# RG-LRU gates with high and low parts stacked in rows, four PSUM buffers and tiles ten blocks apart

## The chip, the cores and the metric

The kernel runs on one core of a Trainium2 chip. The metric is the device time of one execution in microseconds (us), as the median over repeated runs. One core has several engines that work side by side, each through its own list of instructions in a fixed order: PE (matrix products, with weight loads shown as PEld), DVE (elementwise on vectors), ACT (activation functions, copies, casts), POOL (elementwise, slower) and SP, which here only issues DMA transfers. Engines wait for each other through semaphores. PE writes its results into PSUM, a small set of buffers that ACT or DVE must read before they are used again.

## The reference

One step of an encoder with two layers over 544 tokens (512 of a prompt, 32 of a second group), 1024 features. In each layer the input is projected, and three branches follow: softmax attention over chunks (A), retention (B) and a gated linear recurrence (C). Gated merges, a per-layer embedding and a layer norm close the layer. Branch C is what is changed:

```
def rg_lru(xr, s_conv, s_lru, conv_w, conv_b, w_gate_a, b_gate_a, w_gate_x, b_gate_x, lru_lambda):
    ...  # xc: causal convolution of width 4 over xr, plus conv_b; xb: xc in 8 blocks of 64 features
    r = jax.nn.sigmoid((jnp.einsum('btni,nij->btnj', xb, w_gate_a).reshape(b, t, w) + b_gate_a))
    ig = jax.nn.sigmoid((jnp.einsum('btni,nij->btnj', xb, w_gate_x).reshape(b, t, w) + b_gate_x))
    log_a = -LRU_C * r * jax.nn.softplus(-lru_lambda)
    ...  # a = exp(log_a); the input times ig times sqrt(1 - a^2); h = a * h_before + that, along time
```

The branch has 512 features, 8 blocks of 64, and each gate's weights are block-diagonal: a 64 x 64 matrix for each block.

## The kernel before

Activations lie with features in the 128 partitions (rows) and the 544 tokens along the columns. All weights are streamed from memory in blocks of 128 x 128, eight to a DMA (tile `raw`, 512 KB). Products keep nearly full fp32 precision by splitting both sides into a high part and the rest: ACT casts the high part (`wh` of weights, `xh` of activations, function `split` and `hilo`), DVE subtracts it (`wl`, `xl`), and PE adds three products, high x high, high x low, low x high, each in two pieces of 288 and 256 columns, so one block is six matmuls. `stream()` issues casts and subtractions of the blocks up to `LEAD` = 8 ahead of the one in use. SP issues the next `raw` when its buffer is free, which is when DVE's `wl` has read the old one.

The big projections run through a list of blocks in a fixed order. All other work is written as jobs (generators) which the block loop interleaves: each block is a tick, and a job that yields n goes on n ticks later. The table `PACE` holds these distances. So the numbers in `PACE` set the place of each job's instructions between the blocks, the same on each engine, and every engine then runs its list in that order.

Jobs that matter here, in one layer:

- `lru_tile(t)`, t = 0 to 3 (128 features each): convolution (`xc`), its high and low part (`xch`, `xcl`, 128 x 547), then for each of the two gates six matmuls of 274 columns into two PSUM buffers (`sc` and `pv`), and on ACT three sigmoids out of them (`lru_r` for gate a, `lru_i` for gate x). The weights' tile of a gate has two 64 x 64 blocks on the diagonal and zeros elsewhere. POOL multiplies `lru_i` by `xc`.
- `lru_job`, started when tile 3 is done: for four tiles `lru_a` and `lru_r` on ACT (exp, tanh), then three operations on DVE ("trio"), a square root on ACT, a product on POOL, and two scans on DVE (prompt and second group).
- `va_job`/`tok_steps`: the values `VA` are transposed on PE in five "flips" of four transposes each into the PSUM buffer `tp`, and ACT copies each to `vatok`, one flip every three blocks.
- `attn_job`: SP loads two bias tiles (`bias`), POOL masks a corner of each (memset), PE multiplies `KT` and `QT` into `sc`, DVE adds the bias and takes a minimum (`exps`, shown as ISA or CUSTOM_DVE_ANT_0), ACT takes the exponential (`sx`), DVE divides (`norm`), PE transposes into `tp` again. It starts when the gates, `vatok` and the first keys are there.

PSUM has two buffers `mm` for the block products, two `sc`, one `tp` and one `pv`. Before the first block, `busy(WARM)` runs matmuls on zeros, and `ple_split` casts the per-layer embedding (`phl`), whose products come first.

Of the kernel before, what the change touches and what calls it, by code (L numbers as in the profile page):

```python
# [17 lines left out]
NP, NS = 512, 32  # L18
# [37 lines left out]
def blocks_of(kind):  # L56
# [8 lines left out]
LEAD = 8  # L65

HELD = (6, 2)
WARM = 16

PACE = {  # L70
# [5 lines left out]

# [10 lines left out]

P_CW, P_CB, P_BA, P_BX, P_LAM, P_GN, P_LG, P_LB = 0, 16, 20, 24, 28, 32, 36, 44
P_SC, P_SL = 52, 64
P_S0 = 68  # L90
NPAR = P_S0 + 256


# [30 lines left out]
def encoder(ctx: ExitStack, tc, xT, pT, W, RB, KC, VC, PAR, CST, LGB, o_y, o_k, o_v, o_rp, o_rs, o_cv, o_lr):  # L124
# [47 lines left out]

    def tick():
        clock[0] += 1
        stream()
        for j in list(jobs):
            while j[1] <= clock[0]:
                d = next(j[0], None)
                if d is None:
                    jobs.remove(j)  # L180
                    break
                j[1] = clock[0] + d
# [98 lines left out]

    def ple_split(l):
        pr, p2 = ple_in[l]
        for k in range(2):
            hilo(p2[:, k], p2[:, 2 + k], pr[:, k])

    V.memset(zero.bitcast(F32), 0.0)
    busy(WARM)
# [32 lines left out]
    def layer(l, env, nxt):  # L321
        pa = par[l]

        def pcol(c, t):
            return pa[:, c + t:c + t + 1]
# [171 lines left out]

        def lru_tile(t):
            if t == 0:
                env["lru"] = [sl("lru_r"), sl("lru_i"), sl("lru_a")]  # L500
            R, I, _ = env["lru"]
            xrp = env["xrp"]
            xc = tmp("xc", (128, W547))
            S.activation(xc, xrp[:, t, 0:W547], AF.Identity, scale=pcol(P_CW, t), bias=pcol(P_CB, t))
            for j in range(1, 4):
                V.scalar_tensor_tensor(xc, xrp[:, t, j:j + W547], pcol(P_CW + 4 * j, t), xc, MUL, ADD)
            yield PACE["lt1"]
            xch, xcl = (tp_.tile([128, W547], F32R, tag="tmp", name="xch") for _ in range(2))
            hilo(xch, xcl, xc)
            yield PACE["lt2"]  # L510
            for g in range(2):
                w, lo = ([parts[(l * NB + AT["wg"] + g * 4 + t) // 4][i][:, t] for i in range(2)])
                ps = psum("sc"), psum("pv")
                for i, (wg, x) in enumerate(((w, xch), (w, xcl), (lo, xch))):
                    for p_, c0 in ((ps[0], 0), (ps[1], W547 - 274)):
                        T.matmul(p_[:, :274], lhsT=wg, rhs=x[:, c0:c0 + 274], start=i == 0, stop=i == 2)  # L516
                d = (I if g else R)[:, t]
                b_ = pcol(P_BX if g else P_BA, t)
                S.activation(d[:, :274], ps[0][:, :274], AF.Sigmoid, bias=b_)
                S.activation(d[:, 274:NP], ps[1][:, 1:NP - 273], AF.Sigmoid, bias=b_)  # L520
                S.activation(d[:, NP:], ps[1][:, 274 - NS:274], AF.Sigmoid, bias=b_)
                yield PACE["lt3"]
            G.tensor_tensor(I[:, t, :NP], I[:, t, :NP], xc[:, :NP], MUL)
            G.tensor_tensor(I[:, t, NP:], I[:, t, NP:], xc[:, NP + 3:], MUL)
            if t == 3:
                env["gates"] = True
                add(lru_job())

        def lru_job():
            R, I, A = env["lru"]  # L530

            for t in range(4):
                S.activation(A[:, t], R[:, t], AF.Exp, scale=sp[:, 1, l, t:t + 1])
                S.activation(R[:, t], R[:, t], AF.Tanh, scale=sp[:, 0, l, t:t + 1])
                yield PACE["lru0"]
            y = I
            for t in range(4):
                r, a = R[:, t], A[:, t]
                V.scalar_tensor_tensor(r, a, 1.0, r, ADD, MUL)
                V.tensor_scalar(a, r, -1.0, 1.0, MUL, ADD)  # L540
                V.scalar_tensor_tensor(r, a, 1.0, r, ADD, MUL)
                yield PACE["lru1"]
            for t in range(4):
                S.activation(R[:, t], R[:, t], AF.Sqrt)
                yield PACE["lru2"]
            for t in range(4):
                G.tensor_tensor(R[:, t], R[:, t], I[:, t], MUL)
                yield PACE["lru3"]
                V.tensor_tensor_scan(y[:, t, :NP], A[:, t, :NP], R[:, t, :NP], 0.0, MUL, ADD)
                V.tensor_tensor_scan(y[:, t, NP:], A[:, t, NP:], R[:, t, NP:], pcol(P_SL, t), MUL, ADD)  # L550
            yield 2
            env["yc"] = y
            Q.dma_start(out=o_lr[l, :, :, 0:1], in_=y[:, :, NP - 1:NP])
            Q.dma_start(out=o_lr[l, :, :, 1:2], in_=y[:, :, N - 1:N])
# [290 lines left out]
        def evac(kind, t, ps, hf=None):  # L845
# [36 lines left out]
            elif kind == "xr":  # L882
                if t == 0:
                    env["xrp"] = xrp = sl("xrp", shape=(128, 4, N + 6))
                    V.memset(xrp[:, :, 0:3], 0.0)
                    V.tensor_copy(xrp[:, :, NP + 3:NP + 6], pa[:, P_SC:P_SC + 12].rearrange("p (a b) -> p a b", a=4))
                xrp = env["xrp"]
                S.copy(xrp[:, t, 3:3 + NP], pv[:, :NP])
                S.copy(xrp[:, t, NP + 6:], pv[:, NP:])  # L889
                if t == 3:  # L890
                    Q.dma_start(out=o_cv[l, :, :, 0:3], in_=xrp[:, :, NP:NP + 3])
                    Q.dma_start(out=o_cv[l, :, :, 3:6], in_=xrp[:, :, NP + NS + 3:NP + NS + 6])
                add(lru_tile(t), PACE["lt00"] if t == 1 else PACE["lt0"])
            elif kind in ("za", "zb", "zc"):
                for f in {"za": ("ya1", "ya2"), "zb": ("yb",), "zc": ("yc",)}[kind]:
                    need(env, f)
                y = env["y" + kind[1]]
                if t == 0:
                    env[kind] = (sl(kind + "h", F32R), sl(kind + "l", F32R))
                h, lo = env[kind]  # L900
                z = tmp("z")
                S.activation(z, pv, AF.Sigmoid)  # L902
                if kind == "zb":
                    V.scalar_tensor_tensor(z, pv, pcol(P_GN, t), z, MUL, MUL)
                else:
                    V.tensor_tensor(z, pv, z, MUL)
                V.tensor_tensor(z, z, y[:, t], MUL)
                hilo(h[:, t], lo[:, t], z)
            elif kind[0] == "g":
                sg = tmp("sg")  # L910
                S.activation(sg, pv, AF.Sigmoid)  # L911
                env["sg", t] = sg
            elif kind[0] == "b":
                sg = env.pop(("sg", t))
                a, b = t // 4, t % 4
                if kind == "bC":
                    if b == 0:
                        env["m", a] = sl("m")
                    V.tensor_tensor(env["m", a][:, b], pv, sg, MUL)
                else:  # L920
                    V.tensor_tensor(sg, pv, sg, MUL)  # L921
                    m = env["m", a][:, b]
                    (V if kind == "bB" and t == 7 else G).tensor_tensor(m, m, sg, ADD)  # L923
                    if kind == "bB":
                        if b == 0:
                            env["mh", a], env["ml", a] = sl("mh", F32R), sl("ml", F32R)
                        hilo(env["mh", a][:, b], env["ml", a][:, b], m)
            elif kind == "pl":
                if t % 4 == 0:
                    env["ple", t // 4] = sl("ple")  # L930
                S.copy(env["ple", t // 4][:, t % 4], pv)  # L931
            elif kind == "wo":
                a, b = t // 4, t % 4
                if b == 0:
                    env["r", a] = sl("r")
                r, xh_, xl_ = env["r", a][:, b], st["xh"][a][:, b], st["xl"][a][:, b]
                V.scalar_tensor_tensor(r, xh_.bitcast(F32), ALPHA, pv, MUL, ADD)
                V.scalar_tensor_tensor(r, xl_.bitcast(F32), ALPHA, r, MUL, ADD)  # L938
                hilo(xh_, xl_, r)
            elif kind == "pg":  # L940
                if t == 7 and hf and l == L - 1:
                    for _ in gate(t, ps, hf):
                        pass
                else:
                    add(gate(t, ps, hf), 0)
# [92 lines left out]

    with tc.manual_schedule():
        envs = [{} for _ in range(L + 1)]  # L1040
        stream(2)
        ple_split(0)
        add(x_job(envs[0]), PACE["x"])
        for l in range(L):
# [84 lines left out]
```

## Time and profile before

| | |
|---|---|
| median of 3 runs | 1309.9 us (1309.42 to 1310.03) |
| profiled execution | 1309.81 us, span 1308.0 |
| PE busy | 1291.7 us, 10744 matmuls |
| DVE busy | 717.3 us |
| ACT busy | 546.1 us |
| POOL busy | 177.0 us |
| matmuls of the gates (line 516) | 96, in both layers |
| HBM read | 112.57 MB |

The span is the time from the first to the last instruction of the profiled execution. A row of the timeline gives start, duration, engine, line, operation, output <- inputs with the tile's shape, and in brackets the idle time before it with what ended it. Rows of equal kind that follow each other are drawn together (x2, x3).

### The profile page before, as it was taken

The numbers are of one execution on the slowest core, as the hardware profiler recorded it, in microseconds if no ns is written. First come the engines' busy times: TensorE is split into PE (matmuls) and PEld (weight loads), VectorE is DVE, ScalarE is ACT, GpSimd is POOL, SyncE is SP. The second block draws the span as 40 slices with busy tenths as digits, with TensorE's granted clock in tenths as the row PEclk, the third lists the DMA queues.
The fourth block names the chain that finished last, engine by engine and source line by source line (L and its number), as shares of the span: only waits on it lengthen the run. The fifth ranks groups of instructions, "written<-read, shape, count | busy, mean of one in ns | idle before, by whom it ended". The sixth has DMA issues, their size and how long they took to land.

```text
span 1308.0 us, 25456 instructions
## 1 busy us (share of the span) xinstructions
PE 1291.7 (99%) x10744; PEld 1263.5 (97%) x10744; DVE 717.3 (55%) x1271; ACT 546.1 (42%) x1065; POOL 177.0 (14%) x158
## 2 busy tenths in 40 slices
PE   9999999999999999999999999999999999999996
PEld 9999999999999999999989998999999999999996
DVE  5666662573753453465584756626637444434567
ACT  6665544323632232333277655443235322332231
POOL 0210120410101201000032201224001011010000
PEclk9999999999999999999999999999999999999998
DMA  7233522231222222224112335222222222222231
GB/s 282 66 131 98 171 69 80 85 105 50 85 93 82 97 68 94 97 97 146 65 49 66 131 99 166 74 83 82 89 66 81 95 83 86 92 81 97 81 113 69
DMA packets 43457, 125.90 MB, mean 96 GB/s; under 512 B 9360, under 2 KB 11664, under 8 KB 42576
## 3 DMA queue, kind: packets, MB, share of 16 engines
q1 hardware_dynamic: 43344, 124.29, 28.8%
q8 instruction: 84, 1.38, 0.4%
q14 instruction: 29, 0.24, 0.1%
HBM read 112.57 MB, written 7.24 MB: 92 GB/s over the span
## 4 chain that ended last, share of the span: by engine, by line
PE 95%; DVE 3%; DMA 1%; ACT 1%; issue 0%; SPq 0%; POOL 0%; DVEq 0%
PE mm L254 84%; PE pv L432 2%; PE sc L402 2%; PE tp L418 1%; PE tp L330 1%; DMA raw<-in_W 1%; PE sc L661 1%; PE pv L684 1%; PE pv L516 0%; DVE r L813 0%; PE sc L516 0%; DVE xl L263 0%; PE sc L744 0%; PE sc L597 0%; PE pv L679 0%
## 5 line engine op out<-in xcount | busy, mean ns | idle before, releaser
L254 PE MATMUL mm<-xh,wh 128*128 128x288 f32 x2144 | 455.5, 294 | 0.4 <-ACT xrp L889 0.4
L254 PE MATMUL mm<-xh,wl 128*128 128x288 f32 x2144 | 444.1, 288 | 0.0
L254 PE MATMUL mm<-xl,wh 128*128 128x288 f32 x2144 | 442.7, 288 | 0.0
L210 DVE TENSOR_TENSOR wl<-raw,wh 128x512 fp32r<-128x512 f32 (+1 forms) x354 | 261.4, 756 | 283.8 <-ACT wh L209 279.9
L254 PEld LDWEIGHTS mm<-xh,wh 128*128 128x128 f32 x2144 | 328.3, 189 | 10.7 <-issue 7.4
L254 PEld LDWEIGHTS mm<-xl,wh 128*128 128x128 f32 x2144 | 328.8, 188 | 0.0
L254 PEld LDWEIGHTS mm<-xh,wl 128*128 128x128 f32 x2144 | 328.5, 188 | 0.2 <-DVE wl L210 0.2
L209 ACT CAST wh<-raw 128x512 fp32r<-128x512 f32 (+1 forms) x354 | 208.3, 614 | 36.9 <-PE mm L254 30.8
L911 ACT ACTIVATE sg<-mm 128x544 f32<-128x544 f32 x48 | 30.1, 626 | 154.1 <-PE mm L254 154.1
L923 POOL TENSOR_TENSOR m<-m,sg 128x544 f32<-128x544 f32 x30 | 46.8, 1560 | 316.6 <-DVE sg L921 316.6
L355 ACT ACTIVATE sx<-sx,sst 128x128 f32<-128x128 f32 (+4 forms) x68 | 38.0, 559 | 70.1 <-DVE sst L353 66.0
L254 PE MATMUL mm<-xh,held 128*128 128x288 f32 (+1 forms) x320 | 64.0, 291 | 0.3 <-ACT ple L931 0.3
L254 PE MATMUL mm<-ml,wh 128*128 128x288 f32 (+1 forms) x256 | 52.9, 288 | 0.0
L254 PE MATMUL mm<-mh,wl 128*128 128x288 f32 (+1 forms) x256 | 52.6, 286 | 0.0
L254 PE MATMUL mm<-mh,wh 128*128 128x288 f32 (+1 forms) x256 | 52.5, 286 | 0.0
L254 PEld LDWEIGHTS mm<-xh,held 128*128 128x128 f32 x320 | 51.3, 188 | 0.6 <-ACT ple L931 0.5
L254 PE MATMUL mm<-xl,held 128*128 128x288 f32 (+1 forms) x160 | 46.4, 290 | 0.5 <-DVE xl L263 0.5
L262 ACT CAST xh<-r 128x544 fp32r<-128x544 f32 (+2 forms) x32 | 17.0, 532 | 67.8 <-DVE r L938 63.6
L921 DVE TENSOR_TENSOR sg<-mm,sg 128x544 f32<-128x544 f32 x32 | 23.2, 725 | 36.7 <-PE mm L254 36.7
L565 POOL TENSOR_TENSOR swap<-swap,cst 128x544 f32<-128x544 f32 x16 | 25.3, 1580 | 109.8 <-DMA swap<-QB 68.1
L902 ACT ACTIVATE z<-mm 128x544 f32<-128x544 f32 x24 | 15.0, 626 | 59.2 <-PE mm L254 59.1
L254 PEld LDWEIGHTS mm<-mh,wl 128*128 128x128 f32 x256 | 39.3, 188 | 0.0
(251 smaller groups left out, 1791.9 us busy)
## 6 DMA issues: line engine op xcount, KB each, us to landing
raw<-in_W SPq DMA_DIRECT2D x189, 512.0 KB, 3.3
bias<-in_RB SPq DMA_DIRECT2D x16, 256.0 KB, 4.1
x<-in_xT SPq DMA_DIRECT2D x4, 544.0 KB, 9.2
o_v<-VA SPq DMA_DIRECT2D x2, 1088.0 KB, 5.1
o_k<-KT SPq DMA_DIRECT2D x2, 1088.0 KB, 5.1
swap<-KB SPq DMA_DIRECT2D x32, 68.0 KB, 2.0
swap<-QB SPq DMA_DIRECT2D x32, 68.0 KB, 2.0
o_y<-tk SPq DMA_DIRECT2D x6, 256.0 KB, 2.1
```

What stands on the lines that cost most here:

```text
L209: S.copy(h[:, k:k + step], t)
L210: V.tensor_tensor(lo[:, k:k + step], t, h[:, k:k + step].bitcast(F32), SUB)
L254: T.matmul(ps[:, MM0 + a:MM0 + b], lhsT=w[:, n % 4, :], rhs=x[:, a:b], start=first and i == 0, stop=last and i == 2)
L262: S.copy(h, src)
L355: S.activation(x, x, AF.Exp, bias=s[:, 0:1], scale=-1.0, accum_out=s[:, 1:2])
L402: T.matmul(scs[j][:, o:o + n], lhsT=q_[r, p, i * 128:i * 128 + 128], rhs=k_[r, p, :n], start=k == 0, stop=k == 2)
L432: T.matmul(pv[64 * j:64 * j + 64, i * 128:i * 128 + 128], lhsT=env["vatok"][:, kt, h * 64:h * 64 + 64], rhs=xs[j][:, o:o + 128], start=kt ...
L565: G.tensor_tensor(sw, sw, cst[:, C_SIN:C_SIN + N], MUL)
L902: S.activation(z, pv, AF.Sigmoid)
L911: S.activation(sg, pv, AF.Sigmoid)
L921: V.tensor_tensor(sg, pv, sg, MUL)
L923: (V if kind == "bB" and t == 7 else G).tensor_tensor(m, m, sg, ADD)
```

## The change

The gates' weights are laid out densely: for each block of 64 features one tile holds [gate a | gate x] side by side (64 x 128), twice below each other in the rows. On the other side the rows are the high part of one half of a tile's features and the low part of the same half. One matmul then adds high x high and low x high in one pass, and with the weights' low part it adds the rest. A tile needs, for each half, two matmuls in two pieces: 8 instead of 12. Half 0 goes to the two `sc` buffers, half 1 to `pv` and `tp`. Each PSUM buffer now holds gate a in 64 rows and gate x in the other 64, so ACT reads it in pieces of 64 rows, 8 for a tile instead of 6; the cast and the subtraction of `xc` also go in two halves of 64 rows. All tiles of the recurrence are 547 columns wide (the three between the two groups are carried along), and POOL's product is one instead of two.

`PACE` puts the tiles about ten blocks apart and has `lru_job` go on every 2 ticks, not 3. At the start, weights are cast at most two blocks ahead for the first eight blocks, `WARM` is 14, and the first embedding half is cast in two pieces.

```
-WARM = 16
+WARM = 14
...
-    "sa3": 3, "lt0": 2, "lt00": 8, "lt1": 8, "lt2": 5, "lt3": 3, "lru0": 3, "lru1": 3, "lru2": 1, "lru3": 3,
+    "sa3": 3, "lt0": (2, 13, 15, 17), "lt1": 8, "lt2": 5, "lt3": 3, "lru0": 2, "lru1": 2, "lru2": 1, "lru3": 3,
...
-        stream()
+        stream(LEAD if clock[0] > 8 else 2)
...
         for k in range(2):
-            hilo(p2[:, k], p2[:, 2 + k], pr[:, k])
+            for a, b in SPANS if l == 0 and k == 0 else ((0, N),):
+                hilo(p2[:, k, a:b], p2[:, 2 + k, a:b], pr[:, k, a:b])
...
-            xch, xcl = (tp_.tile([128, W547], F32R, tag="tmp", name="xch") for _ in range(2))
-            hilo(xch, xcl, xc)
+            xs = [tp_.tile([128, W547], F32R, tag="tmp", name="xhl") for _ in range(2)]
+            rows = slice(0, 64), slice(64, 128)
+            for b in range(2):
+                S.copy(xs[b][rows[b]], xc[rows[b]])
+            for b in range(2):
+                V.tensor_tensor(xs[b][rows[1 - b]], xc[rows[b]], xs[b][rows[b]].bitcast(F32), SUB)
             yield PACE["lt2"]
-            for g in range(2):
-                w, lo = ([parts[(l * NB + AT["wg"] + g * 4 + t) // 4][i][:, t] for i in range(2)])
-                ps = psum("sc"), psum("pv")
-                for i, (wg, x) in enumerate(((w, xch), (w, xcl), (lo, xch))):
+            for b in range(2):
+                n = l * NB + AT["wg"] + 2 * t + b
+                ps = [psum(k) for k in (("pv", "tp") if b else ("sc", "sc"))]
+                for i in range(2):
                     for p_, c0 in ((ps[0], 0), (ps[1], W547 - 274)):
-                        T.matmul(p_[:, :274], lhsT=wg, rhs=x[:, c0:c0 + 274], start=i == 0, stop=i == 2)
-                d = (I if g else R)[:, t]
-                b_ = pcol(P_BX if g else P_BA, t)
-                S.activation(d[:, :274], ps[0][:, :274], AF.Sigmoid, bias=b_)
-                S.activation(d[:, 274:NP], ps[1][:, 1:NP - 273], AF.Sigmoid, bias=b_)
-                S.activation(d[:, NP:], ps[1][:, 274 - NS:274], AF.Sigmoid, bias=b_)
+                        T.matmul(p_[:, :274], lhsT=parts[n // 4][i][:, n % 4], rhs=xs[b][:, c0:c0 + 274],
+                                 start=i == 0, stop=i == 1)
+                for d, r, b_ in ((R, rows[b], P_BA), (I, rows[1 - b], P_BXS)):
+                    b_ = pcol(b_, t)[r]
+                    S.activation(d[rows[b], t, :274], ps[0][r, :274], AF.Sigmoid, bias=b_)
+                    S.activation(d[rows[b], t, 274:], ps[1][r, 1:274], AF.Sigmoid, bias=b_)
                 yield PACE["lt3"]
-            G.tensor_tensor(I[:, t, :NP], I[:, t, :NP], xc[:, :NP], MUL)
-            G.tensor_tensor(I[:, t, NP:], I[:, t, NP:], xc[:, NP + 3:], MUL)
+            G.tensor_tensor(I[:, t], I[:, t], xc, MUL)
...
-                add(lru_tile(t), PACE["lt00"] if t == 1 else PACE["lt0"])
+                add(lru_tile(t), PACE["lt0"][t])
...
-        stream(2)
+        stream(1)
         ple_split(0)
```

How the instructions move, counted in blocks from a layer's first: the gate products stood in groups of six at blocks 46, 49, 52, 54, 55, 57, 62 and 65; they stand in groups of four at 46, 49, 57, 60, 67, 70, 77 and 80. The flips stay at 84, 87, 90, 93 and 96, the first attention products at 105, the transposes of softmax weights at 113, 116 and 121.

On ACT, at the first flips, before (`vatok<-tp` is the copy of a flip; the numbers tell buffers apart):

```order
L533 ACTIVATE lru_a_474<-lru_r_472,sp_92 128x544
L534 ACTIVATE lru_r_472<-lru_r_472,sp_92 128x544
L855 COPY VA_746<-mm_913 128x544
L209 CAST wh_981<-raw_798 128x512
L209 CAST wh_1012<-raw_798 128x512
L331 COPY vatok_1021<-tp_1023 128x512
L331 COPY vatok_1021<-tp_1050 128x512
L879 ACTIVATE QTh_1062<-mm_980 128x544
```

And in the changed order, from the copy of flip 0 on, behind the second pair of `lru_a` and `lru_r`:

```order
L335 COPY vatok_1003<-tp_1005 128x512
L542 ACT_TABLE_LOAD
L542 ACTIVATE lru_a_474<-lru_r_472,sp_92 128x547
L543 ACTIVATE lru_r_472<-lru_r_472,sp_92 128x547
...
L335 COPY vatok_1003<-tp_1033 128x512
L888 ACTIVATE QTh_1045<-mm_957 128x544
L890 ACTIVATE qs_1047<-mm_957 128x32
L211 CAST wh_1053<-raw_842 128x512
```

The table load and the pairs of all four tiles stood ahead of the flips' copies; now they stand between them: tiles 0 and 1 between copies 0 and 1, tile 2 between copies 1 and 2, tile 3 between copies 2 and 3.

On DVE, from the keys' low part (`KTl`) to the first softmax (ISA), before:

```order
L263 TENSOR_TENSOR KTl_1149<-KT_1146,KTh_1148 128x544
L860 COPY kn_1065<-mm_1069 128x32
L210 TENSOR_TENSOR wl_1155<-raw_950,wh_1154 128x512
L210 TENSOR_TENSOR wl_1191<-raw_950,wh_1190 128x512
L549 SCALAR_TENSOR_TENSOR lru_i_473<-lru_a_474,lru_r_472 128x512
...
L880 SCALAR_TENSOR_TENSOR QTl_1063<-mm_1153,QTh_1062 128x544
L210 TENSOR_TENSOR wl_1236<-raw_1016,wh_1235 128x512
L353 ISA sx_1249,sst_1263<-sc_1247,bias_1200 128x128
```

And in the changed order (`raw_919` there is what `raw_950` was):

```order
L265 TENSOR_TENSOR KTl_1136<-KT_1133,KTh_1135 128x544
L869 COPY kn_1048<-mm_1052 128x32
L212 TENSOR_TENSOR wl_1142<-raw_919,wh_1141 128x512
L548 SCALAR_TENSOR_TENSOR lru_r_472<-lru_a_474,lru_r_472 128x547
L549 TENSOR_SCALAR lru_a_474<-lru_r_472 128x547
L550 SCALAR_TENSOR_TENSOR lru_r_472<-lru_a_474,lru_r_472 128x547
...
L212 TENSOR_TENSOR wl_1182<-raw_919,wh_1181 128x512
L889 SCALAR_TENSOR_TENSOR QTl_1046<-mm_1140,QTh_1045 128x544
L212 TENSOR_TENSOR wl_1225<-raw_1001,wh_1224 128x512
L357 ISA sx_1239,sst_1253<-sc_1237,bias_1189 128x128
```

All four trios stood ahead of `KTl`; now those of tiles 0 and 1 stand just ahead of it and those of tiles 2 and 3 ahead of the second `wl`. The scans of tiles 0 and 1, which stood ahead of the softmax, now come in the places of tiles 2 and 3, and the scans of tiles 2 and 3 ahead of the next pair's weights.

SP's list at the bias tables, in the changed order:

```order
L203 DMA raw_1001<-in_W 128x1024
L203 DMA raw_1095<-in_W 128x1024
L203 DMA raw_1185<-in_W 128x1024
L347 DMA bias_1189<-in_RB 128x512
L347 DMA bias_1191<-in_RB 128x512
L203 DMA raw_1284<-in_W 128x1024
```

It reads as before, and nothing moved here: the bias tables stand behind the `raw` that takes the buffer of `raw_919` (of `raw_950` before), and so behind DVE's last `wl` from it.

More of the change, by code (lines that the diff above doesn't have):

```diff
@@ L89 @@
 P_SC, P_SL = 52, 64
-P_S0 = 68
+P_BXS = 68
+P_S0 = 72
 NPAR = P_S0 + 256
@@ L499, in lru_tile @@
             if t == 0:
-                env["lru"] = [sl("lru_r"), sl("lru_i"), sl("lru_a")]
+                env["lru"] = [sl(k, shape=(128, 4, W547)) for k in ("lru_r", "lru_i", "lru_a")]
             R, I, _ = env["lru"]
@@ L535, in lru_job @@
                 yield PACE["lru0"]
-            y = I
+            y = I[:, :, :N]
             for t in range(4):
@@ L549, in lru_job @@
                 V.tensor_tensor_scan(y[:, t, :NP], A[:, t, :NP], R[:, t, :NP], 0.0, MUL, ADD)
-                V.tensor_tensor_scan(y[:, t, NP:], A[:, t, NP:], R[:, t, NP:], pcol(P_SL, t), MUL, ADD)
+                V.tensor_tensor_scan(y[:, t, NP:], A[:, t, NP + 3:], R[:, t, NP + 3:], pcol(P_SL, t), MUL, ADD)
             yield 2
@@ L1068 @@
             if kind == "wg":
-                W[l, n // 8, :, n % 8] = 0
-                for b in range(2):
-                    r = slice(64 * b, 64 * b + 64)
-                    W[l, n // 8, r, n % 8, r] = g["w_gate_x" if k // 4 else "w_gate_a"][l, 2 * (k % 4) + b]
+                ax = [g[a][l, k] for a in ("w_gate_a", "w_gate_x")]
+                W[l, n // 8, :, n % 8] = np.tile(np.concatenate(ax[::-1] if k % 2 else ax, 1), (2, 1))
                 continue
@@ L1094 @@
             put(c, feat(g[k][l], t))
+        put(P_BXS, np.roll(feat(g["b_gate_x"][l], 4), 64, 0))
         put(P_SC, feat(g["state_conv"][l, 0], 4))
```

## The prediction

> **What bounds the kernel now.** I read the page's head, clock row and chain first, then the timelines of the three places that the change touches.
>
> ```profile
> span 1308.0 us, 25456 instructions
> PE 1291.7 (99%) x10744; PEld 1263.5 (97%) x10744; DVE 717.3 (55%) x1271; ACT 546.1 (42%) x1065; POOL 177.0 (14%) x158
> PEclk9999999999999999999999999999999999999998
> PE 95%; DVE 3%; DMA 1%; ACT 1%; issue 0%; SPq 0%; POOL 0%; DVEq 0%
> ```
>
> PE is busy for 99% of the span and carries 95% of the chain. Two things follow: a matmul that is taken away is worth its own time, and a new wait of PE is paid in full, since there is no slack left to swallow it. The profiled execution took 1309.81 us, 0.1 below the median of 1309.9, with 1.8 outside the span; I sum against 1309.8.
>
> **The start.** Timeline from the beginning (start, duration, engine, line, what; in brackets the idle time before and its releaser):
>
> ```profile
> 1.20 4.00 PE L269 MATMUL mm<-zero 128*128 128x272 f32 x16 [1.20 <-DVE eps L289]
> 4.59 1.30 ACT L262 CAST phl<-pr 128x544 fp32r<-128x544 f32 x2
> 5.29 1.52 PE L254 MATMUL mm<-phl,wh 128*128 128x288 f32 x4
> 7.62 0.71 ACT L209 CAST wh<-raw 128x256 fp32r<-128x256 f32 x2 [1.74 <-DMA raw<-in_W]
> 8.87 0.62 ACT L209 CAST wh<-raw 128x512 fp32r<-128x512 f32 x1 [0.53 <-DMA raw<-in_W]
> 9.40 1.12 ACT L931 COPY ple<-mm 128x544 f32<-128x544 f32 x2
> 10.05 0.77 PE L254 MATMUL mm<-phl,wh 128*128 128x288 f32 x4 [0.71 <-ACT ple L931]
> 11.68 0.72 DVE L263 TENSOR_TENSOR xl<-x,xh 128x544 fp32r<-128x544 f32 x1
> ```
>
> The first product at 5.29 waits for a cast of 544 columns (half of the 1.30 at 4.59); with the cast cut in two it needs the first piece, about 0.3 sooner, and two warm-up matmuls fewer (4.00 / 16 = 0.25 each) are out of the way by then. At 10.05 PE waits for ple, whose copy stood on ACT behind a weight cast that waited for its DMA. With weights two blocks ahead that cast comes behind the copy, which can start when the pair at 7.62 is done (8.33); this takes away the 0.71, up to 0.9 with the weight load's part. Later weights, cast nearer to their use, can cost small waits where a DMA lands late: I put 0.2 against it. Gain 1.0; bounds 0.3 (the first cast alone) and 1.2.
>
> **The gate products.** PE in the middle of a tile's second gate, and the wait that the answer for line 516 lists (total, times):
>
> ```profile
> 52.76 0.29 PE L516 MATMUL sc<-xch,held 128*128 128x274 f32 x1
> ...
> 53.27 0.42 PE L254 MATMUL mm<-xh,wh 128*128 128x288 f32 x2
> ```
>
> ```profile
>   ACT lru_r L521: 0.6, 2
> ```
>
> From 52.76 to 53.27 four matmuls pass, 0.128 each. 32 of the 96 go: 4.1. Twice a gate waited for ACT to read the other gate's buffer; with four buffers and tiles ten blocks apart (7.5 us at six matmuls of 0.126) these 0.6 go too. Gain 4.7, bounds 4.1 and 4.7. Against this a tile costs ACT one more cast and eight sigmoid pieces for six, DVE one subtraction more. The table by stretch (PE, PEld, DVE, ACT, POOL busy) around the gates:
>
> ```profile
> 34.00:64.00 30.00, 29.90 (x238) 29.69 (x236) 18.97 (x33) 19.93 (x47) 5.96 (x6) 1.00 0.24 71
> ```
>
> No row shows 547 columns on 64 partitions; the bounds are half and all of the 128-partition prices, 0.65 and 0.72, and I take all. With some 1.3 for the sigmoids that is 2 us of ACT and 0.7 of DVE a tile, once in 7.5 us, where ACT idles 10 of 30 us and DVE 11. I cost it at nothing; without that cover it would be 2 us a tile at most. Sum so far -5.7, or 1304.1, if nothing new waits.
>
> **What moves.** Tile 3 of the recurrence now finishes at block 80 instead of 65. The work behind it (lru_a and lru_r on ACT, three DVE operations a tile, then root, product, scan) starts where PE transposes VA, one flip every three blocks from 84 to 96. PE's own places of flips and attention stay. F is flip 0's start on PE, 77.46.
>
> ```profile
> 69.64 0.75 ACT L533 ACTIVATE lru_a<-lru_r,sp 128x544 f32<-128x544 f32 x1
> 72.50 0.60 ACT L209 CAST wh<-raw 128x512 fp32r<-128x512 f32 x1
> 77.46 0.60 PE L330 MATMUL tp<-cst,VA 128*128 128x128 f32 x4
> 78.09 0.59 ACT L331 COPY vatok<-tp 128x512 f32<-128x512 f32 x1 [1.79 <-PE tp L330]
> 81.55 0.63 ACT L879 ACTIVATE QTh<-mm 128x544 fp32r<-128x544 f32 x1 [0.16 <-PE mm L254]
> 82.85 0.60 PE L330 MATMUL tp<-cst,VA 128*128 128x128 f32 x4
> 85.12 1.28 ACT L544 ACT_TABLE_LOAD   x1
> ```
>
> *Step 1, the flips.* tp has one buffer, so flip n+1 waits for ACT's copy of flip n. On ACT there now stand between copy 0 and copy 1 a table load (1.28) and the lru pairs of two tiles (72.50 - 69.64 = 2.86). Copy 0 ends at F+1.2, the load F+2.5, the pairs F+5.4, copy 1 F+6.0. Flip 2 stands at 82.85 - 77.46 = 5.4 and waits 0.65. Then QTh, QTl on DVE, qs and a cast (to F+8.0), tile 2's pair (F+9.4), copy 2 (F+10.0). Flip 3 stands at 8.1 + 0.65 and waits 1.3. Copy 3 ends at F+12.4, flip 4 is due at F+12.7. A layer 1.9, bounds 1.3 (the detour over DVE hidden) and 2.5 (as much more).
>
> *Step 2, the first softmax.* DVE, POOL, SP and PE behind it, and the stretch's busy times:
>
> ```profile
> 76.42 0.72 DVE L539 SCALAR_TENSOR_TENSOR lru_r<-lru_a,lru_r 128x544 f32<-128x544 f32 x1
> 78.29 0.68 DVE L210 TENSOR_TENSOR wl<-raw,wh 128x512 fp32r<-128x512 f32 x1
> 87.22 4.00 POOL L547 TENSOR_TENSOR lru_r<-lru_r,lru_i 128x544 f32<-128x544 f32 x3 [21.16 <-ACT lru_r L544]
> 89.87 1.93 DVE L263 TENSOR_TENSOR KTl<-KT,KTh 128x544 fp32r<-128x544 f32 x1 [2.57 <-ACT KTh L262]
> 91.82 1.28 DVE L210 TENSOR_TENSOR wl<-raw,wh 128x512 fp32r<-128x512 f32 x2
> 93.02 1.21 DVE L549 TENSOR_TENSOR_SCAN lru_i<-lru_a,lru_r 128x512 f32<-128x512 f32 x1
> 93.12 0.33 SPq L201 DMA_DIRECT2D raw<-in_W  x1
> 93.50 0.91 SPq L343 DMA_DIRECT2D bias<-in_RB  x2
> 97.06 0.14 POOL L373 MEMSET bias<- 64x64 f32 x1 [5.84 <-DMA bias<-in_RB]
> 97.71 0.28 DVE L353 CUSTOM_DVE_ANT_0 sx<-sc,bias 128x128 f32<-128x128 f32 x1
> 99.40 1.32 DVE L550 TENSOR_TENSOR_SCAN lru_i<-lru_a,par,lru_r 128x32 f32<-128x32 f32 x1
> 101.81 0.35 DVE L360 TENSOR_SCALAR sx<-sx,sst 128x256 f32<-128x256 f32 x1
> 102.61 0.49 PE L418 MATMUL tp<-cst,sx 128*128 128x128 f32 x3
> 104.77 0.72 DVE L263 TENSOR_TENSOR KTl<-KT,KTh 128x544 fp32r<-128x544 f32 x1
> ```
>
> ```profile
> 77.40:110.20 32.80, 32.80 (x268) 32.04 (x267) 26.43 (x56) 19.44 (x40) 6.56 (x6) 1.00 0.32 109
> ```
>
> SP issues raw at 93.12, as soon as DVE's wl (91.82, x2) is done, and the bias table behind it. The table lands 3.56 after its issue (memset at 97.06) and the softmax starts. In the changed order the wl that SP waits for stands behind all four trios of the recurrence, and the first trio behind a wl whose cast ends at F+11.9 (ACT: copy 2, tile 3's pair, the cast). So: wl F+12.6; two trios of 78.29 - 76.42 = 1.87 each, F+16.3; KTl, kn, wl, F+17.7; two trios, F+21.4; wl, F+22.1; the bias issue F+22.5; landing F+26.0; softmax F+26.2. The first of POOL's four products falls beside the trios. KTl took 1.93 beside POOL's row at 87.22 and 0.72 alone at 104.77, so a meeting costs 1.2 at most; I add 1.0: F+27.2. From the softmax's start to normalised weights it was 97.71 to 102.16 (end of the row at 101.81), 4.45, with one meeting in it (the small scan at 99.40). Ready at F+31.7. PE's transposes stand at 102.61 - 77.46 = 25.15, with step 1 at 27.1. Wait 4.6; bounds 2.5 (no meeting at all) and 6.8 (the other products all meet DVE here).
>
> [...]
>
> *Step 3, the second softmax.*
>
> ```profile
> 108.02 0.69 DVE L210 TENSOR_TENSOR wl<-raw,wh 128x512 fp32r<-128x512 f32 x1 [1.35 <-ACT wh L209]
> 110.23 0.49 PE L418 MATMUL tp<-cst,sx 128*128 128x128 f32 x3
> ```
>
> Between the first weights and the third set DVE has two more scans, 1.3 each (1.21 and the small piece). One fills the 1.35 in which DVE waited at 108.02; the other delays the weights by 1.3, to 8.3 behind the first, where PE stands 110.23 - 102.61 = 7.6 behind. Wait 0.7; bounds 0 and 2.9 (two meetings).
>
> For meetings beyond those counted I take one, 1.1, in step 2 or 3. A layer 1.9 + 4.6 + 0.7 + 1.1 = 8.3, both 16.6. With no meeting besides the scan's it is 1.9 + 3.6 + 0.7 = 6.2, 12.4; with one more than I take 9.4, 18.8. Against -5.7 that is +10.9, or +6.7 and +13.1: 1320.7, between 1316.5 and 1322.9. Layer 2 has the same order and I price it alike. The rest (547 columns for 544, one POOL product for two, parameters 4 columns wider) is within 0.1 either way, on engines that idle there.
>
> **Rivals.** About 0.2%, 2.6 us, is what a measurement of this kernel can tell from no change.
> - *Nothing new waits* (faster): 1304.1. ACT would have to be through tiles 0 and 1 when copy 1 is asked for, and the bias issued where it is now. It decides where SP's wl ends before F+16.5, 5.6 sooner than I have it. Against it: DVE was busy for 26.4 of these 32.8 us already.
> - *Only the flips wait*: SP waits for an earlier wl than I read from the order, so the bias comes in time: 1304.1 + 3.8 = 1307.9, within 0.2%.
> - *The clock falls* in step 2's wait. The start has the price: 0.25 for 272 columns against 0.128 for 274 later, in a warm-up of 4.00. Four us at that pace lose 2 a layer, 3 with what follows: 1325 to 1327. Against it stands the clock row, full but for the end; but no PE gap of such length is in it.
>
> [...]
>
> **Chances.** My forecast 0.68, its own range 1316 to 1324; the clock 0.12; flips alone, or a small step 2, 0.10; nothing waits 0.10. A range from 1309 to 1327 leaves out the last and half of the third. Faster 0.1, same 0.1, slower 0.8.
>
> **What would show it.** Right: PE idle before flips 2 and 3, released by the copy of vatok, 0.65 and 1.3; one wait of 4 to 6 before the first transposes of softmax weights, released by DVE; the bias issue at F+22 to F+24; no wait at gate products; a first product near 5.0 and none waiting at 10. Wrong: a bias issue before F+18, lru of tiles 0 and 1 ahead of copy 0, or PE waiting at weight products for wh or wl, which I price at nothing because blocks are cast eight ahead (6 us).

## The result and the profile after

The changed kernel takes 1327.0 us (median, 1326.3 to 1327.8) against 1309.7 before in the same comparison: ratio 1.0131, 95% interval 1.0119 to 1.0143, 1.3% slower. The profiled execution took 1326.3. The head, the chain by engine and PE's waits of the profile after:

```profile
span 1324.5 us, 25421 instructions
PE 1292.7 (98%) x10710; PEld 1262.3 (95%) x10710; DVE 728.7 (55%) x1280; ACT 564.2 (43%) x1090; POOL 172.5 (13%) x150
PE 89%; DVE 6%; ACT 2%; DMA 1%; issue 1%; POOL 0%; DVEq 0%; SPq 0%; ACTq 0%
```

```profile
PE tp L422 <- DVE sx L364: 13.0, 3, 6.3
PE tp L334 <- ACT vatok L335: 3.0, 4, 1.0
PE mm L256 <- ACT ple L940: 0.3, 1, 0.3
```

Two waits are new: PE for the softmax weights (13.0 us in three) and for the copies of the flips (3.0 in four). The share of PE in the chain fell from 95% to 89%, that of DVE doubled. The wait at the gate products is gone, and of the 1.0 for `ple` 0.3 is left.

PE's own marks in the first layer after (transposes of VA, then of softmax weights):

```profile
74.06 0.60 PE L334 MATMUL tp<-cst,VA 128*128 128x128 f32 x4
...
80.09 0.66 PE L334 MATMUL tp<-cst,VA 128*128 128x128 f32 x4 [0.47 <-ACT vatok L335]
84.02 0.66 PE L334 MATMUL tp<-cst,VA 128*128 128x128 f32 x4 [1.01 <-ACT vatok L335]
...
107.38 1.15 PE L422 MATMUL tp<-cst,sx 128*128 128x128 f32 x3 [6.09 <-DVE sx L364]
...
113.22 0.49 PE L422 MATMUL tp<-cst,sx 128*128 128x128 f32 x3
...
117.62 0.52 PE L422 MATMUL tp<-cst,sx 128*128 128x128 f32 x3
```

These and the same rows before and in layer 2 split the whole loss. F is again the start of flip 0, "third set" the transposes at 117.62 (110.23 before):

| stretch on PE | before | after | difference |
|---|---|---|---|
| start to F, layer 1 | 77.5 | 74.1 | -3.4 |
| F to first softmax transposes | 25.15 | 33.3 | +8.2 |
| from there to the third set | 7.6 | 10.2 | +2.6 |
| to F of layer 2 | 615.2 | 612.7 | -2.6 |
| the same two stretches in layer 2 | 25.2, 7.6 | 33.6, 10.2 | +8.4, +2.6 |
| to PE's last instruction | 540.5 | 541.2 | +0.7 |

So the gains came (-6.0 in two rows) and 21.8 were lost between the flips and the third set of softmax weights, 10.8 to 11.0 a layer.

ACT at the flips, and DVE, POOL and SP up to the first weights:

```profile
75.30 1.28 ACT L542 ACT_TABLE_LOAD   x1
79.47 0.57 ACT L335 COPY vatok<-tp 128x512 f32<-128x512 f32 x1
83.40 0.57 ACT L335 COPY vatok<-tp 128x512 f32<-128x512 f32 x1
```

```profile
92.42 1.49 DVE L549 TENSOR_SCALAR lru_a<-lru_r 128x547 f32<-128x547 f32 x1
96.47 0.68 DVE L212 TENSOR_TENSOR wl<-raw,wh 128x512 fp32r<-128x512 f32 x1
97.56 0.90 SPq L347 DMA_DIRECT2D bias<-in_RB  x2
101.11 0.14 POOL L377 MEMSET bias<- 64x64 f32 x1 [7.51 <-DMA bias<-in_RB]
101.29 0.29 DVE L357 CUSTOM_DVE_ANT_0 sx<-sc,bias 128x128 f32<-128x128 f32 x1 [1.31 <-POOL bias L377]
101.98 5.26 POOL L556 TENSOR_TENSOR lru_r<-lru_r,lru_i 128x547 f32<-128x547 f32 x3
102.99 1.29 DVE L559 TENSOR_TENSOR_SCAN lru_i<-lru_a,par,lru_r 128x32 f32<-128x32 f32 x1
104.20 1.84 DVE L212 TENSOR_TENSOR wl<-raw,wh 128x512 fp32r<-128x512 f32 x1
106.15 1.17 DVE L364 TENSOR_SCALAR sx<-sx,sst 128x128 f32<-128x128 f32 x1
107.43 0.35 DVE L364 TENSOR_SCALAR sx<-sx,sst 128x256 f32<-128x256 f32 x1
114.96 0.69 DVE L212 TENSOR_TENSOR wl<-raw,wh 128x512 fp32r<-128x512 f32 x1 [1.35 <-ACT wh L211]
```

The softmax starts at F + 27.2, after the bias. From there three rows are longer by 1.0 (the scan's small piece), 1.2 (wl) and 0.9 (the first division), all beside POOL's three products. And the table by stretch, whose third column from the right is the granted clock:

```profile
104.00:107.40 3.40, 0.02 (x1) 0.03 (x1) 3.36 (x5) 0.00 (x0) 3.24 (x3) 0.72 0.13 30
109.00:111.00 2.00, 2.00 (x11) 1.56 (x8) 1.93 (x7) 1.97 (x5) 0.27 (x2) 0.50 0.54 207
112.00:113.00 1.00, 1.00 (x9) 1.00 (x9) 1.00 (x2) 0.00 (x0) 0.00 (x0) 0.85 0.00 0
```

The granted clock falls to a half (0.50) at about 105.5, during the wait, and comes back at about 112.3. From the first transposes to the second PE takes 5.84 in layer 1 and 5.36 in layer 2, before 3.50 in both. The slow clock of the third rival is there, together with the forecast.

### The profile page after: what moved, and what is told of

The parts are those of the page before. It is cut to its first block, busy times and chain, and to the rows that moved or that the text cites. A ratio compares the mean times of both kernels' runs of the same rounds, so it can differ in the third digit from the quotient of the medians.

```text
span 1324.5 us, 25421 instructions
## 1 busy us (share of the span) xinstructions
PE 1292.7 (98%) x10710; PEld 1262.3 (95%) x10710; DVE 728.7 (55%) x1280; ACT 564.2 (43%) x1090; POOL 172.5 (13%) x150
## 4 chain that ended last, share of the span: by engine, by line
PE 89%; DVE 6%; ACT 2%; DMA 1%; issue 1%; POOL 0%; DVEq 0%; SPq 0%; ACTq 0%
PE mm L256 80%; PE pv L436 2%; PE sc L406 1%; PE tp L422 1%; DVE wl L212 1%; PE tp L334 1%; PE sc L670 1%; PE pv L693 1%; DMA bias<-in_RB 1%; DMA raw<-in_W 0%; DVE lru_a L549 0%; DVE lru_i L558 0%; PE sc L753 0%; PE sc L606 0%; ACT lru_a L542 0%
## 5 line engine op out<-in xcount | busy, mean ns | idle before, releaser
L212 DVE TENSOR_TENSOR wl<-raw,wh 128x512 fp32r<-128x512 f32 (+1 forms) x354 | 265.3, 766 | 282.3 <-ACT wh L211 279.1
L422 PE MATMUL tp<-cst,sx 128*128 128x128 f32 x160 | 26.6, 279 | 13.1 <-DVE sx L364 13.0
L256 PEld LDWEIGHTS mm<-mh,wh 128*128 128x128 f32 x256 | 39.3, 188 | 0.0
```

The source lines that it names most:

```text
L212: V.tensor_tensor(lo[:, k:k + step], t, h[:, k:k + step].bitcast(F32), SUB)
L256: T.matmul(ps[:, MM0 + a:MM0 + b], lhsT=w[:, n % 4, :], rhs=x[:, a:b], start=first and i == 0, stop=last and i == 2)
L422: T.transpose(tp[:, c:c + 128], xs[j][:, c:c + 128], ident)
```

## The experiments

All times are medians; the kernel before took 1309.7 to 1310.0 beside them.

**The start alone.** The diff's four edits that touch the start (14 warm-up matmuls, weights at most two blocks ahead, one block ahead of the first embedding, its cast in two pieces) on the kernel before.

> The kernel before with the start alone changed (14 warm-up matmuls, first weights two blocks ahead, first embedding half cast in two pieces). Forecast's term: 1.0 us less than before, 1308.7. Rival, that later weight casts give it back: 1309.7.

Measured 1309.7, ratio 1.0001 (0.9992 to 1.0010). The executions spread from 1308.9 to 1311.5, four of eleven above 1311. The profile is of one at 1311.5; its PE and its granted clock:

```profile
5.20 1.21 PE L254 MATMUL mm<-phl,wh 128*128 128x288 f32 x4 [0.65 <-ACT phl L262]
6.93 0.52 PE L254 MATMUL mm<-phl,wh 128*128 128x288 f32 x2 [0.26 <-ACT phl L262]
7.69 0.82 PE L254 MATMUL mm<-phl,wh 128*128 128x288 f32 x2 [0.24 <-DVE phl L263]
```

```profile
7.00:8.00 1.00, 0.76 (x3) 0.54 (x4) 0.64 (x1) 0.00 (x0) 0.00 (x0) 0.80 0.94 370
8.00:9.00 1.00, 1.00 (x5) 1.00 (x5) 0.00 (x0) 0.00 (x0) 0.00 (x0) 0.50 1.02 400
```

The clock goes to a half (0.50) at about 7.6 and is back at 11, and what the earlier start won is lost (flip 0 at 78.80, 77.46 before). The three short waits alone don't explain it: the profile of the version with POOL's products behind their roots, below, has waits of 0.41, 0.44 and 0.24 at the same places and a full clock (1.00 in every stretch up to 16).

**The start with 16 warm-up matmuls.**

```diff
-WARM = 14
+WARM = 16
```

> The kernel before with the changed start, but the old 16 warm-up matmuls. If the two missing warm-up matmuls make the early gaps of PE long enough to halve the clock in some executions, all executions now lie together, 0.6 to 1.0 below before: 1308.7 to 1309.1. If the later weight casts cause it, the executions stay spread over 1309 to 1311.

Measured 1309.2, ratio 0.9995 (0.9987 to 1.0004), eleven executions between 1308.4 and 1309.8. The group above 1311 is gone: none of eleven, against four of eleven with 14 (the kernel before, with 16, had one of fifteen at 1311.4 beside the start alone). The profiles of all versions point the same way: with 14 the clock falls to a half at 7.6 to 7.8 in three of nine, and in a fourth PE's rows keep their half pace (0.66 for two matmuls, 0.41 later) until about 10 at a granted 1.00; with 16 the clock falls there in none of five. So the two matmuls left out most likely make the start a matter of luck; the counts are small, and the mechanism is not shown. The gain itself, 0.6, is too small to tell from none.

**The gate tiles at the old distances.**

```diff
-"lt0": (2, 13, 15, 17), ... "lru0": 2, "lru1": 2
+"lt0": (2, 8, 2, 2), ... "lru0": 3, "lru1": 3
```

> The changed kernel with the gate tiles at the old distances (groups at blocks 46 to 65) and the recurrence every 3 ticks as before. If the loss comes from where the recurrence falls, both waits of the softmax and of the flips and the slow clock go: about 1304, up to 1305 if the crowded tiles wait for PSUM. If the dense products or the four buffers cost the time, it stays above 1318.

Measured 1317.6 (ratio 1.0059): neither. PE's waits and one of them:

```profile
PE sc L525 <- ACT lru_i L530: 6.6, 2, 3.5
PE tp L422 <- DVE sx L364: 0.2, 1, 0.2
```

```profile
54.25 1.27 PE L525 MATMUL sc<-xhl,held 128*128 128x274 f32 x4 [3.46 <-ACT lru_i L530]
```

With the recurrence back in its place the softmax's wait is gone, 13.0 to 0.2 (25.15 from F to the first transposes, as before). But the gates now wait for ACT, 3.5 in a layer, with the clock at a half behind it (0.50 from 56 to 58). So the place costs the time at the softmax, and the new gates can't stand in the old place: a tile takes ACT eight sigmoid pieces and two casts.

**The tiles somewhat closer.**

```diff
-"lt0": (2, 13, 15, 17)
+"lt0": (2, 10, 10, 8)
```

> The changed kernel with the gate tiles closer (groups at blocks 46, 54, 62, 68 instead of 46, 57, 67, 77), so that the recurrence starts about 9 blocks earlier, ahead of the flips. If the place of the recurrence is what costs the time, the waits at the flips and at the softmax go and a little stays at the gates where ACT is late: 1304 to 1308. If the gates need the full ten blocks, the crowding costs 3 to 5 us a layer as in the run with the old distances: 1311 to 1317.

Measured 1315.3 (1.0043). Again the softmax doesn't wait. The gates wait for DVE's subtraction, which waits for ACT's casts, and the flips for copies that stand behind the recurrence:

```profile
PE tp L334 <- ACT vatok L335: 3.9, 4, 1.1
PE sc L525 <- DVE xhl L518: 3.3, 4, 1.1
```

**The order of before, with the new gates.** Gate groups at 46, 53, 60, 66, and the convolution's first step on DVE to relieve ACT.

```diff
-"lt0": (2, 13, 15, 17), ... "lru0": 2, "lru1": 2        WARM = 14
+"lt0": (2, 9, 8, 6), ... "lru0": 2, "lru1": 3           WARM = 16
-            S.activation(xc, xrp[:, t, 0:W547], AF.Identity, scale=pcol(P_CW, t), bias=pcol(P_CB, t))
+            V.tensor_scalar(xc, xrp[:, t, 0:W547], pcol(P_CW, t), pcol(P_CB, t), MUL, ADD)
```

> The changed kernel with gate groups at blocks 46, 53, 60, 66, the recurrence's DVE work every 3 ticks, 16 warm-up matmuls, and the first step of the convolution on DVE instead of ACT (0.45 for 0.85 us a tile). On ACT and DVE the recurrence then stands between flips and softmax in the order of the kernel before, with dense products and four buffers. If place alone cost the time, no wait at the flips and the softmax is left: 1304 to 1307, with at most 1.5 a layer at the gates. If ACT's longer list at the gates (eight sigmoid pieces, two casts) can't be had in six or seven blocks, waits of 1 to 3 us a layer stay there: 1308 to 1312.

Measured 1312.6 (1.0020, 1.0011 to 1.0029): the best of the versions with dense gates, still slower than before.

```profile
PE tp L334 <- ACT vatok L335: 2.7, 2, 1.4
PE sc L525 <- DVE xhl L518: 2.5, 2, 1.3
```

A layer loses 1.3 at the first gate and 2.0 from F to the first transposes (27.2 against 25.15). Of these, 1.35 is PE's wait for a flip's copy: QTl on DVE stands behind three trios, and ACT waits for it ahead of that copy.

**Two trios ahead of QTl instead of three.** As the last, with `lru1` 4 and tile 0's first step on ACT.

> The kernel of the run before last (order kept: gate groups at 46, 53, 60, 66) with two changes: tile 0's first step of the convolution back on ACT, and the recurrence's DVE work every 4 ticks, so that two and not three of its trios stand ahead of QTl. If tile 0's late operands (1.33 us a layer) and the trio ahead of QTl (1.35 at a flip) are what is left, both go: 1307, 0.2% below before. If the third trio is then late for the softmax, one of them comes back there: 1310 to 1312.

Measured 1320.0 (1.0081), above both readings. The flips no longer wait, but the softmax does:

```profile
PE tp L422 <- DVE sx L364: 6.6, 2, 3.6
```

```profile
92.98 1.74 DVE L212 TENSOR_TENSOR wl<-raw,wh 128x512 fp32r<-128x512 f32 x1 [3.15 <-ACT wh L211]
95.14 2.12 SPq L347 DMA_DIRECT2D bias<-in_RB  x2
99.76 0.29 DVE L357 CUSTOM_DVE_ANT_0 sx<-sc,bias 128x128 f32<-128x128 f32 x1 [1.62 <-POOL bias L377]
```

The wl for which SP waits came late once more (its cast stood on ACT behind the roots), and with it the bias and the softmax: the same path as in the forecast's step 2, by another cause. Tile 0's wait at the gates stayed, so the place of its first step was not its cause.

**The bias loads one weight load earlier** (`bias_loads(0)` moved to the top of `attn_job`).

> The changed kernel with SP's bias loads placed one weight load earlier. If DVE's own order is the bound behind it, the softmax starts 1.3 us a layer sooner, when its weight subtraction is done: 1324.4. If the late bias is the main loss, it gives back most of the 6 us a layer: about 1316. If neither, 1327.

Measured 1322.9 (1.0102), 4.1 less than the changed kernel. But not in the way that was expected: the masks now come early, so POOL's products run beside the trios and not behind the softmax. It starts later, at F + 28.1, when DVE is through its list, and its weights are ready 3.7 later instead of 6.5. So the bias came last in the changed kernel (DVE waited 1.31 for it), but it was not the only bound. PE also waits 1.5 a layer for a `wl` that stands behind the lengthened trios.

**POOL's products right behind their roots.**

```diff
                 S.activation(R[:, t], R[:, t], AF.Sqrt)
                 yield PACE["lru2"]
+                G.tensor_tensor(R[:, t], R[:, t], I[:, t], MUL)
             for t in range(4):
-                G.tensor_tensor(R[:, t], R[:, t], I[:, t], MUL)
                 yield PACE["lru3"]
```

> The changed kernel with POOL's four products each right behind its root, ahead of the bias masks. If POOL and DVE shut each other out, the 3.1 us of longer DVE rows between the softmax and its division go, and one or two meetings (1.0 each) come in front of the bias issue instead: 1 to 2 us a layer less, 1323 to 1325, the clock still halved. If the meetings don't set the wait, 1327.

Measured 1326.7 (1.0128), not told apart from 1327.0. The softmax takes 3.1 less to its weights (3.4 instead of 6.5), and DVE's rows among the trios are longer instead, so it starts 2.2 later:

```profile
93.45 1.50 DVE L549 TENSOR_SCALAR lru_a<-lru_r 128x547 f32<-128x547 f32 x1
94.98 1.77 DVE L550 SCALAR_TENSOR_TENSOR lru_r<-lru_a,lru_r 128x547 f32<-128x547 f32 x1
```

The rows take 0.45 and 0.73 alone, so each meeting cost 1.0 here. It was paid on DVE's way to the softmax instead of behind it.

**PE kept busy in the wait.**

```diff
+            if p == 0 and qs == (0, 1):
+                fill = psum("tp")
+                for _ in range(40):
+                    T.matmul(fill[:, :H2], lhsT=zero[:, :128], rhs=zero, start=True, stop=True)
```

> The changed kernel with 40 matmuls on zeros on PE ahead of the first softmax's transposes in each layer (no part of the computation; 5.0 us at full clock inside an idle 6.1). If the idle time halves the clock and the halved clock costs 2.3 us a layer, 1322.3. If the slow rows are no loss or have another cause, 1327.

Measured 1328.9 (1.0145, executions 1326.5 to 1330.7), nothing gained. PE in layer 1:

```profile
103.51 5.18 PE L422 MATMUL tp<-zero 128*128 128x272 f32 x40
110.11 0.81 PE L426 MATMUL tp<-cst,sx 128*128 128x128 f32 x3 [1.42 <-DVE sst L363]
114.10 0.49 PE L426 MATMUL tp<-cst,sx 128*128 128x128 f32 x3
120.23 0.66 PE L426 MATMUL tp<-cst,sx 128*128 128x128 f32 x3 [1.86 <-DVE sx L364]
```

Up to the third set the clock held (1.00 from 96 to 118): 110.11 to 114.10 is 4.0 against 5.8. But the third set is no earlier, 10.1 after the first against 10.2: what the clock gave back turned into 1.86 of waiting for DVE.

The total says less than this stretch, for the clock fell all the same, only later:

```profile
118.00:122.00 4.00, 2.14 (x19) 1.61 (x17) 3.15 (x10) 1.22 (x3) 0.00 (x0) 0.81 0.55 136
```

Behind the wait of 1.86 it is at a half from about 120.5 to 123.9, and the next set comes 6.0 after the third instead of 4.5. In layer 2 it is at a half from 769 to about 772.4, behind a wait of 1.60 for the first set, and the second set comes 5.4 after the first, as without the filling. This execution also has the slow start (F is 76.43, 74.06 in the changed kernel's).

**The scans 12 ticks later** (`yield 12` between the roots and the products).

> The changed kernel with POOL's products and the scans of the recurrence 12 ticks later, so that no scan stands ahead of the first two sets of softmax weights (the products still meet DVE, on POOL right behind the bias masks). If DVE's list from the trios to the second set of weights is the bound, 2.4 us go in front of the first set and 2 in front of the second, a layer: 1316 to 1319. If the slow clock and not DVE sets the time between the two sets, only the first part goes: 1322.

Measured 1323.2 (1.0104), near the second reading. In layer 1 DVE has the second pair's weights ready at 113.1, and PE comes to them at 116.2, since it still went through the halved clock (0.50 from 105 to 111): from the second transpose of the first set (106.27) to the third set it takes 9.9.

**Both of the last two**: scans later, and 28 matmuls on zeros.

> The run with the scans 12 ticks later, and 28 matmuls on zeros on PE ahead of the first transposes of each layer (no part of the computation; 3.6 us inside an idle 4.6). There DVE is no longer the bound between the two sets of weights, so if the halved clock is what sets that time now, keeping PE busy gives 2.3 us a layer: 1318.5 instead of 1323.2. If filling changes nothing here either, as it did with the scans in place, the slow clock is not the bound: 1323.

Measured 1319.0 (1.0070), 4.1 less than with the scans alone. Here the clock stays full (1.00 from 101 to 111, and 0.997 as the mean of the span, as in the kernel before), and the filling is worth 2 us a layer:

```profile
104.89 0.33 PE L426 MATMUL tp<-cst,sx 128*128 128x128 f32 x1
105.80 0.44 PE L426 MATMUL tp<-cst,sx 128*128 128x128 f32 x2 [0.58 <-DVE sx L364]
...
113.54 0.49 PE L426 MATMUL tp<-cst,sx 128*128 128x128 f32 x3
```

From 105.80 to the third set it is 7.7, as at full clock before (7.6). So between the two sets there were two bounds of nearly the same length. In layer 1 it is 10.1 with the scans in place and a full clock, 9.9 with the scans away and a half clock, 10.2 with both bounds and 7.7 with neither. Taking away one uncovers the other.

**Bias early and scans late together**, with 16 warm-up matmuls.

> The changed kernel with the bias loads one weight load earlier, the scans 12 ticks later and 16 warm-up matmuls. If the two moves (4.1 and 3.8 us less each alone) shorten the same DVE list at different places, they add: 1318 to 1319. If each only uncovers the other's wait, 1322.

Measured 1322.1 (1.0090; executions 1319.6 to 1323.0). The two moves hardly add. With the scan gone from between the softmax and its division, DVE waits 1.56 there for a cast on ACT, so the first transposes stand at F + 31.3, as with the bias alone (31.4). The clock falls in layer 1; in the profiled execution, the fastest of the four, it doesn't fall in layer 2, behind the same wait of 2.48 (mean clock 0.995, 0.992 in the other three). How much each of these holds was not separated.

None of the versions with dense gates is faster than the kernel before. Whether some order of the jobs keeps the gain is open.

## Why the prediction came out as it did

The direction, the place and the chain of waits were right. The size was not: 1327.0 lies at the very end of the range, 6.3 above the forecast and 3 above its own range. That it is also the number of the rival with the slow clock (1325 to 1327) is chance, as the last two steps show. By its steps:

- *The gates*: -4.7 forecast. No wait stands at line 525, and the stretch between the layers' softmaxes, which holds one layer's gates, is 2.6 shorter (half of 4.7 is 2.35). The cover held: ACT is busy 33 of the 40 us around the new gates, and in all four runs with less distance PE waited at the gates.
- *The start*: -1.0 forecast; the profiled execution shows it (flip 0 comes 3.4 earlier, 1.0 more than the gates give), but over many executions it is nothing. The step didn't ask what two warm-up matmuls fewer do to the clock.
- *Step 1*: flips 2 and 3 at F + 6.0 and F + 10.0 forecast, 6.03 and 9.96 measured. Right; the waits drawn in PE's rows are 0.47 and 1.01 for 0.65 and 1.3.
- *Step 2*: softmax at F + 27.2 forecast and measured, the bias issue at F + 23.5 (22 to 24 given). The wait was 6.2, not 4.6 and beyond the 4 to 6 given as a sign: all three remaining products met DVE here, the upper bound's case, where one more (1.1) was taken for both steps together. The bias came last, as forecast, but only by the 1.31 that DVE waited for it; with the bias early POOL's products met the trios, and the softmax started 0.9 later.
- *Step 3*, the term that failed: 0.7 forecast, 2.6 measured. "One fills the 1.35 in which DVE waited" was wrong. The row at 114.96 has the same 1.35 again: the cast that wl waits for stands on ACT behind the exponential, which waits for DVE's own softmax row, and a scan put ahead of that row moves both. An idle time that an engine's own earlier work sets is not room. The softmax row and the cast, before, and the scan with the same two rows after:

```profile
106.11 0.55 DVE L353 CUSTOM_DVE_ANT_0 sx<-sc,bias 128x384 f32<-128x384 f32 x1
107.38 0.61 ACT L209 CAST wh<-raw 128x512 fp32r<-128x512 f32 x1
```

```profile
111.77 1.21 DVE L558 TENSOR_TENSOR_SCAN lru_i<-lru_a,lru_r 128x512 f32<-128x512 f32 x1
113.08 0.53 DVE L357 CUSTOM_DVE_ANT_0 sx<-sc,bias 128x384 f32<-128x384 f32 x1
114.33 0.60 ACT L211 CAST wh<-raw 128x512 fp32r<-128x512 f32 x1
```

- *The clock* was given 0.12 as another case. It fell in both layers (0.50 from 109 to 111 and from 763.9 to 765), and what it took (2.3 in layer 1, 1.9 in layer 2) is in the 2.6 of step 3, not beside it: with the clock kept full DVE's list still held the third set at 10.1, and with the scans away the half clock held it at 9.9.

The sum: 2 x (8.3 + 2.6) = 21.8 lost against 16.6 forecast, where 8.3 and 2.6 are the two stretches of the table. In the forecast's terms a layer has 1.9 + 6.2 + 2.6 = 10.7 against 1.9 + 4.6 + 0.7 + 1.1 = 8.3. The 0.7 behind the third set of layer 2 was not followed up.

In layer 1 of the changed kernel PE was idle from 101.3 to 107.38; the clock was at a half 4.2 after the idle began and full again 4.9 after PE resumed. Other runs differ: the clock was halved behind waits of 1.60 and 1.86 with PE kept busy and of 2.48 with bias and scans moved, and the start alone shows it halved at 7.6 with no single wait over 0.65. So a wait shorter than the 6.09 of the changed kernel is no proof of a full clock here, and what decides it is not shown.

The forecast took the price of a meeting from a row with two tensors, KTl. Beside POOL, TENSOR_SCALAR rows with one tensor went from 0.45 to 1.49 (line 549) and from 0.29 to 1.17 (line 364), so such rows have to be counted as meetings too.

## What to carry to other kernels

Work moved in the program is worth or costs what it does to each in-order queue that it lands in, and to what those queues release: here 32 matmuls fewer gave some 5 us in the profile, and the recurrence that came to stand between flips and softmax cost 21.8. Follow the chain over all engines (DVE's subtraction, the weight load that waits for it, the bias behind that load, the softmax) before pricing a move by its own duration. And before a gap is taken as room, ask whose work ends it: if it is the same engine's, one hop away, it moves along.

## What was new about the hardware

- The halved clock cost only what no other chain covered: from the first to the third set of softmax weights in layer 1 it was 10.1 at full clock behind DVE's longer list, 9.9 at half clock without the scans, 10.2 with both and 7.7 with neither.
- The clock halved behind a wait as short as 1.60 (from 769 in layer 2 of the run with PE kept busy), and the same wait of 2.48 was followed by a half clock in one layer of a run and not in the other.
- With 14 warm-up matmuls the clock was at a half from 7.6 to 7.8 on, until about 11, in three of nine profiles. In these three the 14 had taken 3.35 to 3.45 us, in five others 3.54. With 16 it fell in none of five.
- On 64 partitions ACT's cast of 547 columns took as long as on 128 (1.32 for two, 0.66 for one, line 516 after and 262 before), so splitting by rows doubled ACT's time for it.
